# Row numbers and gates of an expert's slots: summed by TensorE, finished on ScalarE, with turns and sums at other places of the tile loop

## The chip, the cores and the metric

The kernel runs on one core of one Trainium2 chip. The metric is the device time of one execution in microseconds; three runs of the kernel before took 1885.34, 1885.52 and 1890.42 us (median 1885.52).

## The reference

One decoder layer over 512 tokens of width 1024, in float32: a mixing part (retention and dilated attention), then a mixture of experts, then a last RMSNorm. What matters here is the mixture. Each token goes to the top 4 of 32 experts by a softmax router; the gates are the softmax over the four values. An expert is a matrix of 1024x2048, a clamped SwiGLU, and a matrix of 1024x1024, and the results are summed into the tokens with the gates:

```
u   = xb @ w1[e] + b1[e]
glu = minimum(u[:, ::2], 7);  lin = clip(u[:, 1::2], -7, 7)
a   = glu * sigmoid(1.702 * glu) * (lin + 1)
y[row_tok] += (a @ w2[e] + b2[e]) * row_gate
```

## The kernel before, in words

The mixing part, the output projection and the router come first and fill the time up to about 720 us; the 32 experts follow, and after them a loop for overflowing experts (it runs zero times here) and the last norm.

**Slots.** An expert works on slots, each of which holds one token. The two first experts are fixed, the others are sorted by their number of tokens; after that order `KIND` (line 30) gives each place of the loop 96 slots ("L") or 64 ("S"): LLLL, then LS fourteen times. A matmul in float32r of two parts (hi and lo) stands for a float32 product: for L three products a tile (x hi by w hi, x hi by w lo, x lo by w hi), 12 matmuls; for S the hi and the lo part of x lie side by side in 128 columns, so that two products, 8 matmuls, do, and the lower half is added to the upper one by a `fold` (ScalarE copies the lower half, TensorE adds it).

**Tiles.** The loop at line 1318 runs over 384 tiles of 128x2048 float32, 1 MB each: eight of kind "A" (first matrix, k=0 to 7) and four of kind "B" (second matrix, k=0 to 3) an expert. The order is A(e), then B(e-1), then A(e+1), and so on. All engines follow an order written out by hand: each engine executes its instructions in the order of the source. In tile i TensorE multiplies with tile i; then ScalarE makes w_hi of tile i+4 (`prep_hi`, line 1043), VectorE makes w_lo of tile i+3 (`prep_lo`, line 1049) and SyncE issues the load that takes the buffer just freed. There are nine load buffers, five for w_hi and four for w_lo. The other operations of tile i stand behind these two on their engines.

**What else hangs on the tiles** (line numbers of the kernel before):

- `slot_hot` (line 1141, VectorE): a one-hot matrix oh, token by slot, from the rank of each token in the expert. At k=3 (for e=0 at k=0, 2 and 5).
- `slot_sum` (line 1147, TensorE): oh times `aux`, whose columns hold for each token p, 128*t, 1 and three bfloat16 parts of the gate. One matmul of 6 columns for each of the four token tiles, into `psl`. At A k=7 for the expert two ahead.
- `slot_rows` (line 1154): ScalarE copies the six sums to `sl`; POOL computes the row number (an empty slot is sent to a spare row), turns it into an int32 `idx`, issues the gather `xg` of the token rows, and sums the gate's three parts into `gate`.
- `turn` and `turn_copy` (lines 1173 and 1119): TensorE turns 512 columns of the gathered rows `xg` (or of the activations `av`) into a PSUM tile `pt`; ScalarE copies its hi part, VectorE subtracts to get the lo part. `av` of the expert before at k=3 and 4, `xg` of the next one at k=5 and 6. `pt` and `psl` share two buffers.
- `evacuate` (line 1305): for S first the fold; then the sigmoid on ScalarE (`open_gates`), `linear` and `times_glu` on VectorE, which read the one PSUM tile `u`. At B k=0. `times_gate` follows at B k=2.
- `close` (line 1313): ScalarE scales y by the gate into `ys`, POOL issues a DMA that adds the rows to `s_acc` in HBM. At A k=0 of the expert two later.

Of the kernel before, what the change touches and what calls it, by code (L numbers as in the profile page):

```python
# [17 lines left out]
OP = mybir.AluOpType  # L18
# [96 lines left out]
def body(tc, a, out):  # L115
# [679 lines left out]
    rg = rt.tile([P, NT, 2, E], F32, name="rg")  # L795
    rk1 = rg[:, :, 0]
    rkp = rt.tile([P, NT, E], F32, name="rkp")
    aux = rt.tile([P, NT, E, 6], BF, name="aux")
    selb = rt.tile([P, NT, 4, E], BF, name="selb")
    trib = rt.tile([P, 2, P], BF, name="trib")  # L800
    btile = rt.tile([P, TB], F32R, name="btile")
# [4 lines left out]
    V.memset(trib[:, 1], 1.0)  # L806
    V.tensor_copy(aux[:, :, :, 0], misc[:, 256:257].to_broadcast([P, NT * E]).rearrange("p (t e) -> p t e", t=NT))
    for t in range(NT):
        G.memset(aux[:, t, :, 1], float(P * t))
    G.memset(aux[:, :, :, 2], 1.0)  # L810
    s4 = ExitStack()
    psx = ExitStack()
    psB = psx.enter_context(tc.tile_pool(name="psB", bufs=2, space=PSUM, reuse_waits="tile"))
# [144 lines left out]
        A.activation(e4s[:, t0:t1], e4s[:, t0:t1], AF.Exp)  # L958

    def gate_parts(g, rest, s):  # L960
        V.tensor_copy(aux[:, :, s, 3], g)
        V.tensor_tensor(rest, g, aux[:, :, s, 3], op=OP.subtract)
        V.tensor_copy(aux[:, :, s, 4], rest)
        V.tensor_tensor(aux[:, :, s, 5], rest, aux[:, :, s, 4], op=OP.subtract)
# [138 lines left out]
    def slots_of(e):  # L1103
        return CAP if KIND[e] == "L" else SMALL
# [42 lines left out]
    def slot_sum(oh, aux_e):  # L1147
        n = oh.shape[2]
        ps = psC.tile([CAP, 8], F32, name="psl", tag="pt", bufs=2)
        for t in range(NT):  # L1150
            PE.matmul(ps[:n, :6], oh[:, t], aux_e[:, t], start=(t == 0), stop=(t == NT - 1))
        return ps[:n]

    def slot_rows(ps, fetch_rows=True):
        n = ps.shape[0]
        sl = m2.tile([CAP, 10], F32, name="sl")[:n]
        A.activation(sl[:, :6], ps[:, :6], AF.Copy)  # L1157
        G.tensor_scalar(sl[:, 6:7], sl[:, 2:3], misc[:n, 258:259], misc[:n, 257:258], op0=OP.mult, op1=OP.add)  # L1158
        G.tensor_add(sl[:, 7:8], sl[:, 0:1], sl[:, 1:2])
        idx = m2.tile([CAP, 1], I32, name="idx", bufs=4)[:n]  # L1160
        G.tensor_add(sl[:, 9:10], sl[:, 6:7], sl[:, 7:8])
        G.tensor_copy(idx, sl[:, 9:10])
        xg = None
        if fetch_rows:
            xg = m2.tile([CAP, D], F32, name="xg", bufs=1)[:n]
            G.indirect_dma_start(out=xg, out_offset=None, in_=xn2,
                                 in_offset=bass.IndirectOffsetOnAxis(ap=idx[:, :1], axis=0))
        G.tensor_add(sl[:, 8:9], sl[:, 3:4], sl[:, 4:5])
        gate = m2.tile([CAP, 1], F32, name="gate", bufs=4)[:n]
        G.tensor_add(gate, sl[:, 8:9], sl[:, 5:6])  # L1170
# [127 lines left out]
    U, Y, AVS, SG, AT, SL = {}, {}, {}, {}, {}, {}  # L1298
    now = {}
    hot_at = {(0, 0): 1, (0, 2): 0}  # L1300
    hot_at.update({(e, 3 if e else 5): e + 2 for e in range(E - 2)})
    sum_at = {(0, 1): 1, (0, 4): 0}
    sum_at.update({(e, 7): e + 2 for e in range(E - 2)})

    def evacuate(e):
        if KIND[e] == "S":
            fold(U[e], now["low"])
        u = U.pop(e)[:slots_of(e)]
        SG[e] = open_gates(u)
# [7 lines left out]

    for i, (kind, e, k) in enumerate(tiles):
        hi, lo = his.pop(i), los.pop(i)
        nx = sum_at.get((e, k)) if kind == "A" else None  # L1320
        if kind == "A":
            if nx is not None:
                now["ps"] = slot_sum(now["oh"], aux[:, :, nx])
            if e == 0 and k == 1:
                sort_rows()
                rgT = sort_turn()
            if e == 0 and k == 3:
                sort_tables(rgT)
            if e and k in (3, 4):
                now["at", k - 3] = turn(AVS[e - 1], k - 3)  # L1330
            if e + 1 < E and k in (5, 6):
                now["xt", k - 5] = turn(SL[e + 1][2], k - 5)
            if k == 0:
                U[e] = u_tile()
                if KIND[e] == "L":
                    for j in range(4):
                        bias_mm(U[e][:CAP, j], e, j)
            if KIND[e] == "L":
                xh, xl = X[e]
                for s_, m_ in ((xh, hi), (xh, lo), (xl, hi)):  # L1340
                    for j in range(4):
                        PE.matmul(U[e][:CAP, j], s_[:, k], m_[:, j * 512:(j + 1) * 512], start=False,  # L1342
                                  stop=(k == KC - 1 and s_ is xl))
            else:
                for m_ in (hi, lo):
                    for j in range(4):
                        PE.matmul(U[e][:, j], X[e][2][:, k], m_[:, j * 512:(j + 1) * 512], start=(k == 0 and m_ is hi),  # L1347
                                  stop=False, skip_group_check=True)
                    if k == 0 and m_ is hi:
                        for j in range(4):  # L1350
                            bias_mm(U[e][:SMALL, j], e, j, False)
        else:
            if k == 0:
                Y[e] = y_tile()
                if KIND[e] == "L":
                    for n in range(2):
                        bias_mm(Y[e][:CAP, n], e, 4 + n)
                if e == E - 1:
                    for q in range(2):
                        turn_copy(turn(AVS[e], q), slice(4 * q, 4 * q + 4), AT[e])  # L1360
            if KIND[e] == "L":
                ah, al = AT[e]
                for s_, m_ in ((ah, hi), (ah, lo), (al, hi)):
                    for c in range(2):
                        for n in range(2):
                            col = c * 1024 + n * 512
                            PE.matmul(Y[e][:CAP, n], s_[:, 2 * k + c], m_[:, col:col + 512], start=False,  # L1367
                                      stop=(k == 3 and s_ is al and c == 1))
            else:
                for m_ in (hi, lo):  # L1370
                    for c in range(2):
                        for n in range(2):
                            col = c * 1024 + n * 512
                            PE.matmul(Y[e][:, n], AT[e][2][:, 2 * k + c], m_[:, col:col + 512],  # L1374
                                      start=(k == 0 and c == 0 and m_ is hi), stop=False, skip_group_check=True)
                        if k == 0 and c == 0 and m_ is hi:
                            for n in range(2):
                                bias_mm(Y[e][:SMALL, n], e, 4 + n, False)
            if e == 0 and k == 0:
                ld = overflow_list()  # L1380
        prep_hi(i + AHEAD_HI)
        prep_lo(i + AHEAD)
        if kind == "A":
            if nx is not None:
                SL[nx] = slot_rows(now["ps"], nx > 0)
            if e == 0 and k == 0:
                sort_counts()
            if (e, k) in hot_at:
# [3 lines left out]
                AVS[0] = times_gate(SG.pop(0), AVS[0])  # L1392
            if e > 1 and k == 0:
                close(e - 2)
            if e and k in (3, 4):
                if k == 3:
                    AT[e - 1] = at_tiles(e - 1)
                turn_copy(now["at", k - 3], slice(4 * (k - 3), 4 * (k - 3) + 4), AT[e - 1])
            if e + 1 < E and k in (5, 6):
                if k == 5:  # L1400
                    X[e + 1] = x_tiles(e + 1)
                turn_copy(now["xt", k - 5], slice(4 * (k - 5), 4 * (k - 5) + 4), X[e + 1])
            if k == KC - 1:
                if KIND[e] == "S":
                    now["low"] = lower(U[e])
                if e == 0:
                    evacuate(0)
            if e == 3 and k == 2:
                G.dma_start(lb.rearrange("p a b -> p (a b)"), bcast(ld, 0, 4 * E))
            if e == 5 and k == 2:  # L1410
                V.tensor_copy(li, lb[0:1])
        else:
            if e + 1 < E:
                if k == 0:
                    evacuate(e + 1)
                if k == 2:
                    AVS[e + 1] = times_gate(SG.pop(e + 1), AVS[e + 1])
                    if e + 1 == E - 1:
                        AT[e + 1] = at_tiles(e + 1)
# [17 lines left out]
    with tc.For_i(0, extra) as it:  # L1437
# [94 lines left out]
```

## Time and profile before

| what | us |
|---|---|
| median of three runs | 1885.52 |
| the profiled execution | 1888.8 |
| its span, first to last instruction | 1887.0 |
| TensorE busy (matmul) | 1747.2 |
| VectorE busy | 1465.3 |
| ScalarE busy | 1084.0 |
| POOL busy | 651.0 |

The mean granted clock of TensorE is 0.966 of full speed. In the profile PE is TensorE's matmuls and PEld its weight loads (they overlap), DVE is VectorE, ACT is ScalarE, POOL is GpSimd and SP is SyncE, which only issues DMAs. L1178 is line 1178 of the kernel. `out<-in` names the tiles that an instruction writes and reads, `xN` counts the instructions put together in a row. Matmuls are pipelined, so that their durations overlap.

### The profile page before, as it was taken

How to read it: one execution, taken by the hardware profiler on the slowest of the kernel's cores; microseconds unless marked ns; L12 is line 12 of the kernel's file. 1: busy time of each engine (PE TensorE's matmuls, PEld its weight loads, DVE VectorE, ACT ScalarE, POOL GpSimd, SP SyncE). 2: the span in 40 equal slices, each digit the busy share in tenths (PEclk: the TensorE clock that was granted, in tenths of full speed). 3: DMA queues.
4: the chain of work that ended last, by engine and by line, in shares of the span. 5: the costliest groups of instructions: out<-in, count | busy, mean ns of one | idle time of the engine just before them, and what ended most of it. 6: DMA issues, size and time to landing. Idle time of an engine off the chain costs nothing.

```text
span 1887.0 us, 23253 instructions
## 1 busy us (share of the span) xinstructions
PE 1747.2 (93%) x8369; PEld 1327.1 (70%) x8369; DVE 1465.3 (78%) x1490; ACT 1084.0 (57%) x1000; POOL 651.0 (34%) x409
## 2 busy tenths in 40 slices
PE   5989999999999988999979999999999999999992
PEld 3878889888778875776656666666667667667661
DVE  7465535657663567998978998998999989999994
ACT  5232332222222334777867877877787787787781
POOL 2140001001110032022945256744746425844601
PEclk8999999999999998999989999999999999999996
DMA  9613424433573737899989999999999999999983
GB/s 313 165 52 90 112 74 139 149 114 105 150 199 119 243 155 276 313 391 361 391 310 389 370 371 396 377 381 378 386 381 383 384 389 369 399 380 373 383 315 116
DMA packets 207909, 525.47 MB, mean 278 GB/s; under 512 B 12102, under 2 KB 127222, under 8 KB 174896
## 3 DMA queue, kind: packets, MB, share of 16 engines
q1 hardware_dynamic: 197744, 494.99, 71.1%
q0 software_dynamic: 10048, 28.98, 6.3%
q8 instruction: 67, 1.10, 0.2%
q14 instruction: 50, 0.41, 0.1%
HBM read 503.67 MB, written 20.25 MB: 278 GB/s over the span
## 4 chain that ended last, share of the span: by engine, by line
PE 81%; DVE 9%; issue 5%; POOL 2%; DMA 2%; ACT 1%; SPq 0%; DVEq 0%; POOLq 0%; ACTq 0%
PE u L1342 21%; PE y L1367 10%; PE u L1347 8%; PE pp L213 6%; PE pp L215 6%; PE pp L214 6%; PE y L1374 5%; DVE w_lo L1049 3%; PE pp L247 2%; PE pp L245 2%; PE pp L246 2%; PE pt L1178 2%; PE u L1138 1%; POOL s_acc L1219 1%; PE y L740 1%
## 5 line engine op out<-in xcount | busy, mean ns | idle before, releaser
L1049 DVE TENSOR_TENSOR w_lo<-w_moe,w_hi 128x2048 fp32r<-128x2048 f32 x384 | 862.3, 2279 | 16.9 <-ACT sl L1157 10.7
L1043 ACT ACTIVATE w_hi<-w_moe 128x2048 fp32r<-128x2048 f32 x384 | 729.2, 1914 | 203.8 <-PE u L1342 116.2
L1219 POOL DMA_INDIRECT s_acc<-ys,idx x32 | 258.9, 8090 | 251.2 <-ACT ys L1218 235.6
L1342 PE MATMUL u<-w_hi,x 128*96 128x512 f32 x1152 | 317.5, 403 | 0.0
L1342 PEld LDWEIGHTS u<-w_hi,x 128*96 128x96 f32 x1152 | 181.5, 164 | 72.8 <-issue 0.6
L1158 POOL TENSOR_SCALAR sl<-sl,misc 96x1 f32<-96x1 f32 (+1 forms) x32 | 105.8, 3305 | 327.4 <-ACT sl L1157 327.4
L213 PE MATMUL pp<-hTh,w_hl 128*128 128x512 f32 x400 | 160.3, 401 | 0.0
L1342 PE MATMUL u<-w_lo,x 128*96 128x512 f32 x576 | 158.8, 398 | 0.0
L215 PE MATMUL pp<-hTh,w_hl 128*128 128x512 f32 x400 | 156.6, 391 | 0.0
L214 PE MATMUL pp<-hTl,w_hl 128*128 128x512 f32 x400 | 156.5, 391 | 0.0
L1367 PE MATMUL y<-w_hi,at 128*96 128x512 f32 x576 | 151.3, 396 | 0.0
L204 DVE TENSOR_TENSOR w_hl<-w_raw,w_hl 128x1024 fp32r<-128x1024 f32 (+1 forms) x66 | 91.3, 1397 | 72.3 <-ACT w_hl L203 72.3
L1347 PE MATMUL u<-w_hi,x 128*128 128x512 f32 x448 | 136.2, 427 | 0.0
L1347 PE MATMUL u<-w_lo,x 128*128 128x512 f32 x448 | 126.3, 405 | 0.6 <-DVE w_lo L1049 0.6
L1342 PEld LDWEIGHTS u<-w_lo,x 128*96 128x96 f32 x576 | 94.8, 165 | 41.2 <-issue 0.5
L1367 PEld LDWEIGHTS y<-w_hi,at 128*96 128x96 f32 x576 | 91.7, 161 | 44.4 <-issue 5.9
L203 ACT ACTIVATE w_hl<-w_raw 128x1024 fp32r<-128x1024 f32 (+1 forms) x66 | 65.2, 1002 | 70.7 <-PE pp L215 54.1
L278 POOL DMA_DIRECT2D s_mod<-brow x16 | 7.9, 492 | 281.1 <-DVE brow L275 228.4
L1347 PEld LDWEIGHTS u<-w_lo,x 128*128 128x128 f32 x448 | 88.1, 197 | 22.5 <-DVE w_lo L1049 1.2
L1347 PEld LDWEIGHTS u<-w_hi,x 128*128 128x128 f32 x448 | 82.9, 200 | 19.0 <-issue 5.4
L213 PEld LDWEIGHTS pp<-hTh,w_hl 128*128 128x128 f32 x400 | 75.5, 189 | 18.1 <-issue 2.6
L215 PEld LDWEIGHTS pp<-hTh,w_hl 128*128 128x128 f32 x400 | 75.4, 188 | 16.2
(345 smaller groups left out, 2901.9 us busy)
## 6 DMA issues: line engine op xcount, KB each, us to landing
w_moe<-in_w_mlp SPq DMA_DIRECT2D x384, 1024.0 KB, 7.6
w_raw<-in_w_in SPq DMA_DIRECT2D x76, 512.0 KB, 5.4
w_ada<-in_w_ada SPq DMA_DIRECT2D x24, 1024.0 KB, 6.2
w_raw<-in_w_ret_o SPq DMA_DIRECT2D x8, 512.0 KB, 4.4
w_o<-in_w_o SPq DMA_DIRECT2D x4, 1024.0 KB, 4.9
s_acc<-z POOLq DMA_DIRECT2D x5, 512.0 KB, 7.2
xin<-in_x SPq DMA_DIRECT2D x4, 512.0 KB, 6.6
w_raw<-in_w_att_o SPq DMA_DIRECT2D x8, 256.0 KB, 5.9
```

What stands on the lines that cost most here:

```text
L204: eng.tensor_tensor(lo[:, :kc], raw, hi[:, :kc].bitcast(F32), op=OP.subtract)
L213: PE.matmul(ps, hi[:, k], mh[:, k], start=(k == 0), stop=False)
L214: PE.matmul(ps, hi[:, k], ml[:, k], start=False, stop=False)
L215: PE.matmul(ps, lo[:, k], mh[:, k], start=False, stop=(k == kc - 1))
L1043: A.activation(his[i], loaded[i], AF.Copy)
L1049: V.tensor_tensor(los[i], loaded[i], his[i].bitcast(F32), op=OP.subtract)
L1158: G.tensor_scalar(sl[:, 6:7], sl[:, 2:3], misc[:n, 258:259], misc[:n, 257:258], op0=OP.mult, op1=OP.add)
L1219: G.indirect_dma_start(out=acc, out_offset=bass.IndirectOffsetOnAxis(ap=idx[:, :1], axis=0), in_=ys, in_offset=None, compute_op=OP.add)
L1342: PE.matmul(U[e][:CAP, j], s_[:, k], m_[:, j * 512:(j + 1) * 512], start=False, stop=(k == KC - 1 and s_ is xl))
L1347: PE.matmul(U[e][:, j], X[e][2][:, k], m_[:, j * 512:(j + 1) * 512], start=(k == 0 and m_ is hi), stop=False, skip_group_check=True)
L1367: PE.matmul(Y[e][:CAP, n], s_[:, 2 * k + c], m_[:, col:col + 512], start=False, stop=(k == 3 and s_ is al and c == 1))
L1374: PE.matmul(Y[e][:, n], AT[e][2][:, 2 * k + c], m_[:, col:col + 512], start=(k == 0 and c == 0 and m_ is hi), stop=False, skip_group_check ...
```

## The change

`aux` gets nine columns in three groups of three, so that a slot's row number parts, its flag and the gate's parts come to stand in the same three columns: (p, 1, gate part 1), (128*t, 0, gate part 2), (0, 0, gate part 3). TensorE adds the three groups into three sums: row, flag and gate. ScalarE computes the row number of the spare row from the flag, adds the row and writes int32, and copies the gate; POOL only issues the gather. The slot sum moves from A k=7 (expert two ahead) to B k=1 (expert three ahead), the one-hot from k=3 to k=5, the turns to k=2, 3 and k=6, 7. `evacuate` is split: the sigmoid of an L expert stands at the end of its A k=7, ahead of the second turn copy of the next expert's rows; the fold and the sigmoid of an S expert stay at B k=0, and its `linear` and `times_glu` move to B k=1.

```diff
-    aux = rt.tile([P, NT, E, 6], BF, name="aux")
+    aux = rt.tile([P, NT, E, 9], BF, name="aux")
...
-        G.memset(aux[:, t, :, 1], float(P * t))
-    G.memset(aux[:, :, :, 2], 1.0)
+        G.memset(aux[:, t, :, 3], float(P * t))
+    G.memset(aux[:, :, :, 1], 1.0)
+    for c in (4, 6, 7):
+        G.memset(aux[:, :, :, c], 0.0)
...
         for t in range(NT):
-            PE.matmul(ps[:n, :6], oh[:, t], aux_e[:, t], start=(t == 0), stop=(t == NT - 1))
+            for g in range(3):
+                PE.matmul(ps[:n, :3], oh[:, t], aux_e[:, t, 3 * g:3 * g + 3], start=(t == 0 and g == 0),
+                          stop=(t == NT - 1 and g == 2))
...
-        A.activation(sl[:, :6], ps[:, :6], AF.Copy)
-        G.tensor_scalar(sl[:, 6:7], sl[:, 2:3], misc[:n, 258:259], misc[:n, 257:258], op0=OP.mult, op1=OP.add)
-        G.tensor_add(sl[:, 7:8], sl[:, 0:1], sl[:, 1:2])
+        A.activation(sl, ps[:, 1:2], AF.Identity, scale=misc[:n, 258:259], bias=misc[:n, 257:258])
         idx = m2.tile([CAP, 1], I32, name="idx", bufs=4)[:n]
-        G.tensor_add(sl[:, 9:10], sl[:, 6:7], sl[:, 7:8])
-        G.tensor_copy(idx, sl[:, 9:10])
+        A.activation(idx, ps[:, 0:1], AF.Identity, bias=sl)
+        gate = m2.tile([CAP, 1], F32, name="gate", bufs=4)[:n]
+        A.activation(gate, ps[:, 2:3], AF.Copy)
...
-        G.tensor_add(sl[:, 8:9], sl[:, 3:4], sl[:, 4:5])
-        gate = m2.tile([CAP, 1], F32, name="gate", bufs=4)[:n]
-        G.tensor_add(gate, sl[:, 8:9], sl[:, 5:6])
...
-    hot_at.update({(e, 3 if e else 5): e + 2 for e in range(E - 2)})
-    sum_at = {(0, 1): 1, (0, 4): 0}
-    sum_at.update({(e, 7): e + 2 for e in range(E - 2)})
-
-    def evacuate(e):
+    hot_at.update({(e, 5): e + 2 for e in range(E - 2)})
+    sum_at = {("A", 0, 1): 1, ("A", 0, 4): 0, ("A", 0, 7): 2}
+    sum_at.update({("B", e, 1): e + 3 for e in range(E - 3)})
+
+    def open_u(e):
         if KIND[e] == "S":
             fold(U[e], now["low"])
+        SG[e] = open_gates(U[e][:slots_of(e)])
+
+    def close_u(e):
         u = U.pop(e)[:slots_of(e)]
-        SG[e] = open_gates(u)
         AVS[e] = linear(u)
         times_glu(u, AVS[e])
...
-            if e and k in (3, 4):
-                now["at", k - 3] = turn(AVS[e - 1], k - 3)
-            if e + 1 < E and k in (5, 6):
-                now["xt", k - 5] = turn(SL[e + 1][2], k - 5)
+            if e and k in (2, 3):
+                now["at", k - 2] = turn(AVS[e - 1], k - 2)
+            if e + 1 < E and k in (6, 7):
+                now["xt", k - 6] = turn(SL[e + 1][2], k - 6)
...
             if k == KC - 1:
                 if KIND[e] == "S":
                     now["low"] = lower(U[e])
+                else:
+                    open_u(e)
                 if e == 0:
-                    evacuate(0)
+                    close_u(0)
+            if e + 1 < E and k in (6, 7):
+                if k == 6:
+                    X[e + 1] = x_tiles(e + 1)
+                turn_copy(now["xt", k - 6], slice(4 * (k - 6), 4 * (k - 6) + 4), X[e + 1])
...
             if e + 1 < E:
-                if k == 0:
-                    evacuate(e + 1)
+                if k == 0 and KIND[e + 1] == "S":
+                    open_u(e + 1)
+                if k == (KIND[e + 1] == "S"):
+                    close_u(e + 1)
```

## Rows read from the trace of the kernel before

**Rows 1.** The page: busy time, share and instructions of each engine.
```profile
PE 1747.2 (93%) x8369; PEld 1327.1 (70%) x8369; DVE 1465.3 (78%) x1490; ACT 1084.0 (57%) x1000; POOL 651.0 (34%) x409
```

**Rows 2.** Stretches: us; PE, PEld, DVE, ACT, POOL busy; clock; DMA share; GB/s.
```profile
848.40:885.10 36.70, 36.70 (x172) 25.51 (x171) 32.72 (x21) 26.33 (x20) 10.60 (x8) 1.00 0.99 372
...
1391.84:1460.72 68.88, 65.07 (x300) 45.99 (x299) 64.45 (x41) 54.74 (x41) 44.99 (x16) 1.00 1.01 385
1460.72:1530.43 69.71, 66.37 (x300) 47.12 (x299) 64.45 (x41) 54.85 (x41) 26.03 (x16) 0.98 1.00 380
...
1388.30:1410.90 22.60, 18.79 (x91) 13.93 (x90) 22.60 (x15) 19.14 (x16) 12.57 (x2) 1.00 0.99 363
1410.90:1423.70 12.80, 12.80 (x55) 8.43 (x54) 12.09 (x9) 10.46 (x6) 12.08 (x6) 1.00 1.02 397
1423.70:1449.30 25.60, 25.60 (x122) 17.34 (x121) 23.41 (x16) 17.48 (x14) 16.70 (x4) 1.00 1.02 395
1449.30:1457.20 7.90, 7.90 (x36) 6.29 (x35) 6.37 (x5) 7.68 (x5) 3.64 (x7) 1.00 1.02 399
```

**Rows 3.** Waits of TensorE, 885 to 1810 us: total us, times, longest.
```profile
PE pt L1178 <- DVE at L1121: 41.5, 17, 3.3
PE pt L1178 <- DMA xg<-s_h,idx: 7.0, 1, 7.0
```

**Rows 4.** Timeline at A(S): start us, us, engine, instruction, [idle before, releaser].
```profile
1391.49 11.09 DVE L1049 TENSOR_TENSOR w_lo<-w_moe,w_hi 128x2048 fp32r<-128x2048 f32 x5
...
1402.84 0.55 DVE L1121 TENSOR_TENSOR at<-pt,at 128x384 fp32r<-128x384 f32 x1
...
1403.44 0.55 PE L1178 MATMUL pt<-misc,xg 96*128 96x96 f32 x4 [3.34 <-DVE at L1121]
```

**Rows 5.** Timeline at the end of A(L) and in B(S).
```profile
1444.97 0.36 ACT L1120 ACTIVATE x<-pt 128x256 fp32r<-128x256 f32 x1
...
1445.37 0.42 DVE L1121 TENSOR_TENSOR x<-pt,x 128x256 fp32r<-128x256 f32 x1 [0.73 <-ACT x L1120]
...
1446.27 0.31 PE L1151 MATMUL psl<-aux,oh 128*96 128x6 bf16 x4
...
1448.29 0.15 ACT L1157 ACTIVATE sl<-psl 96x6 f32<-96x6 f32 x1
...
1451.34 1.00 ACT L1200 ACTIVATE sg<-u 96x1024 f32<-96x1024 f32 x1
...
1452.24 5.51 ACT L1043 ACTIVATE w_hi<-w_moe 128x2048 fp32r<-128x2048 f32 x3
1452.25 1.00 POOL L1166 DMA_INDIRECT xg<-s_h,idx  x1 [0.56 <-POOL idx L1162]
1452.38 1.22 DVE L1205 TENSOR_SCALAR av<-u 96x1024 f32<-96x1024 f32 x1 [1.49 <-ACT sg L1200]
```

**Rows 6.** Timeline of POOL behind a gather in B(L).
```profile
1418.21 8.56 POOL L1168 TENSOR_TENSOR sl<-sl 64x1 f32<-64x1 f32 x1
```

**Rows 7.** Chain of waits: first matmuls of A(S), and one gather.
```profile
896.18 0.92 PE u L1347 x4
...
940.03 10.83 DMA xg<-s_h,idx
...
970.30 0.93 PE u L1347 x4
...
1804.65 0.93 PE u L1347 x4
```

**Rows 8.** DMA: packets 1391.84 to 1530.43 us; issues, size, median us to landing.
```profile
DMA packets 9721, 53.01 MB, mean 382 GB/s; under 512 B 896, under 2 KB 896, under 8 KB 5615
...
w_moe<-in_w_mlp SPq DMA_DIRECT2D x384, 1024.0 KB, 7.6
s_acc<-ys,idx POOLq DMA_INDIRECT x32, 18.0
xg<-s_h,idx POOLq DMA_INDIRECT x31, 7.4
```

More of the change, by code (lines that the diff above doesn't have):

```diff
@@ L960, in gate_parts @@
     def gate_parts(g, rest, s):
[L961 to L964, printed above, removed]
+        V.tensor_copy(aux[:, :, s, 2], g)
+        V.tensor_tensor(rest, g, aux[:, :, s, 2], op=OP.subtract)
+        V.tensor_copy(aux[:, :, s, 5], rest)
+        V.tensor_tensor(aux[:, :, s, 8], rest, aux[:, :, s, 5], op=OP.subtract)
     def gates(t0, t1):
@@ L1155, in slot_rows @@
         n = ps.shape[0]
-        sl = m2.tile([CAP, 10], F32, name="sl")[:n]
-        A.activation(sl[:, :6], ps[:, :6], AF.Copy)
-        G.tensor_scalar(sl[:, 6:7], sl[:, 2:3], misc[:n, 258:259], misc[:n, 257:258], op0=OP.mult, op1=OP.add)
-        G.tensor_add(sl[:, 7:8], sl[:, 0:1], sl[:, 1:2])
+        sl = m2.tile([CAP, 1], F32, name="sl")[:n]
+        A.activation(sl, ps[:, 1:2], AF.Identity, scale=misc[:n, 258:259], bias=misc[:n, 257:258])
         idx = m2.tile([CAP, 1], I32, name="idx", bufs=4)[:n]
-        G.tensor_add(sl[:, 9:10], sl[:, 6:7], sl[:, 7:8])
-        G.tensor_copy(idx, sl[:, 9:10])
+        A.activation(idx, ps[:, 0:1], AF.Identity, bias=sl)
+        gate = m2.tile([CAP, 1], F32, name="gate", bufs=4)[:n]
+        A.activation(gate, ps[:, 2:3], AF.Copy)
         xg = None
@@ L1319, in body @@
         hi, lo = his.pop(i), los.pop(i)
-        nx = sum_at.get((e, k)) if kind == "A" else None
+        nx = sum_at.get((kind, e, k))
+        if nx is not None:
+            now["ps"] = slot_sum(now["oh"], aux[:, :, nx])
         if kind == "A":
-            if nx is not None:
-                now["ps"] = slot_sum(now["oh"], aux[:, :, nx])
             if e == 0 and k == 1:
@@ L1382, in body @@
         prep_lo(i + AHEAD)
+        if nx is not None:
+            SL[nx] = slot_rows(now["ps"], nx > 0)
         if kind == "A":
-            if nx is not None:
-                SL[nx] = slot_rows(now["ps"], nx > 0)
             if e == 0 and k == 0:
@@ L1394, in body @@
                 close(e - 2)
-            if e and k in (3, 4):
-                if k == 3:
+            if e and k in (2, 3):
+                if k == 2:
                     AT[e - 1] = at_tiles(e - 1)
[L1398 to L1402, printed above, removed]
+                turn_copy(now["at", k - 2], slice(4 * (k - 2), 4 * (k - 2) + 4), AT[e - 1])
             if k == KC - 1:
@@ L1443, in body @@
         V.tensor_scalar(rke, rkp[:, :, ds(sv, 1)].rearrange("p t o -> p (t o)"), bo, None, op0=OP.subtract)
-        axe = m1.tile([P, NT, 6], BF, name="axe")
+        axe = m1.tile([P, NT, 9], BF, name="axe")
         V.tensor_copy(axe, aux[:, :, ds(sv, 1), :].rearrange("p t o c -> p t (o c)"))
```

## The prediction

> **What bounds the kernel now.** I read the busy line first, then busy time stage by stage, then what TensorE waited for, then the order of time around its longest wait, then the chain. The busy line [rows 1] gives TensorE 93% and VectorE 78% of the span, an average over unlike stages. The stages to look at are the experts. With a 96-slot expert after a 96-slot expert, TensorE is busy for 36.70 of 36.70 us and VectorE for 32.72: TensorE bounds. From the fifth expert on, 96-slot (L) and 64-slot (S) experts alternate, and a pair of them takes 68.88 or 69.71 us, of which TensorE works 65.07 or 66.37 and VectorE 64.45 [rows 2]. Neither is full; they take turns at waiting. I write A(L), B(L), A(S), B(S) for the eight tiles of the first and the four of the second projection of each kind; the order is A(L), B(S), A(S), B(L), in 25.60, 7.90, 22.60 and 12.80 us, and only A(S) has TensorE idle: 18.79 of 22.60 [rows 2].
>
> What it waits for is one thing: 41.5 us in 17 waits, turning rows (L1178) until VectorE has made the low part of an earlier turn (L1121) [rows 3]. In order of time [rows 4]: VectorE runs five w_lo back to back from 1391.49 for 11.09 us (2.2 each), then the subtraction for the first turn of the activations at 1402.84, and at 1403.44 TensorE, 3.34 us late, can turn the gathered rows, since the two psl/pt buffers are shared and that subtraction frees the first. VectorE's subtraction for tile k stands behind w_lo of tile k+3; TensorE asks for the buffer two tiles later, so it waits for a w_lo that it doesn't need yet. In every second pair the granted clock is 0.98 instead of 1.00, and those are the pairs of 69.71 us [rows 2].
>
> **The change part by part.** *Turns at k=2, 3 and 6, 7 (before 3, 4 and 5, 6).* A buffer is now asked for four tiles after its last use, when w_lo of the tile in hand must be there anyway. The 3.34 us wait and the two of about 0.24 behind it go. What is late next is VectorE, so I follow its chain. Take T=0 at the start of B(S).
>
> *Sigmoid of L at the end of A, before the second turn copy of the rows.* Before, VectorE waited 1.49 us for it in B(S) k=0 [rows 5]. Now ScalarE at A(L) k=7 runs w_hi, then waits for the end of the tile, then the sigmoid (1.00), and behind it stands the copy of the turned rows (0.36), for which VectorE's subtraction (0.42) waits [rows 5]. That is a new wait: queued behind the sigmoid are that copy and the next w_hi. With 0.2 us from TensorE to ScalarE the subtraction ends at T=1.9; VectorE has by then idled about 2.2 us. w_lo to 4.1, linear 1.22 [rows 5] and glu of the same size 1.22, so glu ends at T=6.5, where before it was 1452.38+2.44-1449.3=5.5.
>
> *From there VectorE has no wait until glu of S,* which now stands at B(L) k=1 (before k=0) and frees the single u tile for the next A(L). The work between: 14 w_lo (4 in B(S), 8 in A(S), 2 in B(L)) of 2.2 = 30.8; linear and glu twice, 4.8; one gate multiply of the size of linear, 1.2; four subtractions for 96 slots at 0.5 from [rows 4], 2.0; one one-hot compare, the 0.26 between the five w_lo and 1402.84, 0.3. Sum 39.1. Then TensorE must run A(L), 25.6 less the 0.2 of the slot sum that leaves it, 25.4 [rows 2, 5], with 0.1 to hand over; then the sigmoid, copy and subtraction close the ring, 0.2+1.00+0.36+0.42=2.0. The ring is 39.1+0.1+25.4+2.0=66.6 us a pair. The two other rings are shorter: VectorE's own work 64.45, TensorE's 65.07+0.7. In this walk TensorE waits some 0.4 us for w_lo in each of the last three tiles of A(S) and 0.9 for u in A(L) k=0, short waits in place of a long one.
>
> *Slot sum in three matmuls a tile, 12 instead of 4.* Four take 0.31 us with their drain [rows 5], at most 0.08 each; eight more are between 0 (if loads overlap) and 0.6. I take 0.04 each, half of it, as the last end is drain: 0.35 an expert. In pairs it lies beside the VectorE ring and costs nothing; its cover is the 0.8 us between TensorE's 65.8 and 66.6, gone if VectorE gets faster. In the L stage it is on the path: 7 sums, 2.4 us.
>
> *Row number and gate on ScalarE.* Six small POOL operations an expert go; one of 0.2 us took 8.56 beside w_lo [rows 6]. They are off the path (POOL 34% busy), except once: 7.0 us of waiting for gathered rows [rows 3], whose gather the chain shows landing late, 10.83 us from 940.03 [rows 7]. ScalarE gets two operations more, like the 0.15 us copy [rows 5]; form and int32 output are not in the trace, so 0.15 to 0.4 each. Hidden: ScalarE is busy 54.74 of 68.88 [rows 2]. They stand at B k=1 behind w_hi, and queued behind them are w_hi and the copies. ScalarE also takes over POOL's wait for the scatter-add of four experts before (idx has four buffers), 18.0 us from issue to landing [rows 8]; nine tiles lie between, 22 us in the walk, so 4 us are spare.
>
> *Three more memsets and a wider aux* run on POOL long before the experts, beside the output projection; 0, below 1 us if seen. One-hot at k=5 feeds a sum four tiles on, as before: 0. *Last experts:* VectorE enters A of the last expert up to 1.0 us later and TensorE waits there already: +1.0.
>
> **Sum.** From 970.30 to 1804.65 are 12 pairs, 69.53 each; the pair before took 74.12 from 896.18 [rows 7]. 12x(69.53-66.6)+(74.12-66.6)=35.2+7.5=42.7 gained, 2.4+1.0 lost: 39.3. The profiled execution took 1888.8 us (span 1887.0 and 1.8 around it), so 1849.5; the median of the runs is 1885.52, 3.3 lower, so 1846.
>
> **The rivals.** *(a) The transfers bound.* Over two pairs the DMA moved 53.01 MB at 382 GB/s [rows 8] and the engines' busy share is already 1.00 to 1.01 [rows 2]. 26.5 MB in 66.6 us asks for 398 GB/s. For it: the share. Against it: at the same share A(L), B(L) and B(S) run at 395 to 399 for 46 us [rows 2], a weight tile lands 7.6 us after issue [rows 8] with nine tiles in the ring, and no wait of ScalarE on a weight transfer shows. Held at 385 GB/s a pair would take 68.9: 12x0.6+5.2-3.4=9 us gained, 1876. The Trainium skill (SBUF — State Buffer, A bandwidth-pool intuition that's wrong) gives about 358 GB/s from HBM to a core; by that a pair would need 74 us, and nothing could be won. The trace does not agree: 382 GB/s are measured [rows 8].
>
> *(b) Slower: the gather for S's partner is shut out.* In B(S) ScalarE ends two w_hi (1.8 apart [rows 5]) and the small ones at T=5.4, and the gather starts 0.3 to 0.6 later, at 5.7 to 6.0. VectorE runs glu until 6.5, and then 6 w_lo and a gate multiply without a break to T=21. Beside linear a gather takes 1.00 us [rows 5], but the POOL operation that stood before a run of w_lo took 8.56 [rows 6]. If the index comes 0.5 us later than worked out, the gather goes out at 21, lands 7.4 later [rows 8] at 28.4, and A(S) k=6 wants it at 22.1: 6.3 us of waiting, less 1.3 of short waits that vanish, so 71.6 a pair: 13x71.6-908.5=+22, with +3.4 some 26 slower, 1911. Before, POOL's small operations waited themselves into the linear window; that shelter goes. The Trainium skill (SBUF — State Buffer, Who interferes with whom) says that a VectorE instruction with two SBUF inputs contends with a GpSimd instruction that reads SBUF, that one with a single SBUF input doesn't, and that the first to issue keeps the port to its end. By that rule a gather begun in glu is safe; the trace agrees as far as 1.00 beside linear and 8.56 beside w_lo go.
>
> *(c) The wait only moves:* VectorE is as late as before, pairs stay at 69.5, and only the 7 us gather wait goes: 1882 to 1885. For it: VectorE ends glu of L 1.0 us later. Against it: its idle time, 4.4 to 5.3 us a pair, has only the 2.2 us at A(L) k=7 left to sit in.
>
> **How the numbers follow.** The ring holds: 0.60, 1834 to 1860 (one us a pair either way is 13 us). (a), wholly or in part: 0.15, 1860 to 1878. (b): 0.16, 1892 to 1915. (c): 0.09, 1879 to 1886. What a measurement can tell from no change is 0.3%, 5.7 us. Faster: the ring and (a), 0.76; same: (c), 0.08; slower: (b) and what else stalls ScalarE, 0.16. The range 1833 to 1880 leaves out (b) and the slow end of (c).
>
> **What would show it.** Right: pairs of 66 to 67 us at clock 1.00; the wait of L1178 on L1121 down from 41.5 to under 10; VectorE waiting some 2 us for the copy at A(L) k=7 and TensorE about 1 us for u in A(L) k=0; L experts 0.3 longer; gathers of 1.0 us. Wrong: waits of TensorE on gathered rows, of ScalarE on weight tiles or on the scatter-add, or pairs of 69 and more.

## The result and the profile after

The changed kernel takes 1854.18 us (median of four runs, 1851.98 to 1856.01) against 1885.43 (1885.19 to 1890.42) for the kernel before on the same chip: a ratio of 0.982, 95% interval [0.981, 0.983]. The profiled execution took 1853.22 us with a span of 1851.4. Forecast were 1846, a range of 1833 to 1880, and 1834 to 1860 for the likeliest case.

The busy line of the page stands against [rows 1]:

```profile
PE 1750.5 (95%) x8625; PEld 1329.4 (72%) x8625; DVE 1457.3 (79%) x1490; ACT 1094.7 (59%) x1064; POOL 349.7 (19%) x220
```

POOL has half its work left; TensorE has 256 small matmuls more. The stretches of the kernel after stand against [rows 2]: one 96-slot expert after another, then pairs from the first matmul of A(S) to the next; the columns are those of [rows 2].

```profile
851.47:888.71 37.24, 37.24 (x180) 25.75 (x179) 32.69 (x20) 26.87 (x22) 13.97 (x2) 1.00 0.99 376
...
900.42:966.48 66.06, 64.79 (x313) 46.62 (x312) 60.53 (x39) 52.39 (x43) 31.85 (x5) 1.00 0.98 372
...
1365.45:1431.93 66.48, 66.05 (x315) 46.57 (x314) 63.99 (x41) 55.49 (x45) 13.23 (x5) 1.00 1.02 397
1431.93:1499.50 67.57, 65.85 (x315) 46.66 (x314) 64.09 (x41) 55.59 (x45) 12.57 (x5) 1.00 1.02 398
1499.50:1568.07 68.57, 67.45 (x315) 47.65 (x314) 64.27 (x41) 55.61 (x45) 14.43 (x5) 0.98 1.02 396
...
1701.02:1767.46 66.44, 65.31 (x303) 46.12 (x302) 63.02 (x40) 54.95 (x42) 11.03 (x4) 1.00 1.02 397
```

Most pairs that took 68.88 to 69.71 take 66.48, at a clock of 1.00. The 13 pairs from 900.42 to 1767.46 take 867.0 us; before they took 908.5 [rows 7]. That is 41.4 us gained. The way to the first pair is 4.4 us longer and the tail behind the last 1.4, which leaves the 35.6 us by which the spans differ.

What TensorE waits for, 885 to 1810 us (against [rows 3]), and under it the same of VectorE and ScalarE:

```profile
PE u L1195 <- ACT low L1190: 3.7, 4, 1.5
PE pt L1178 <- DVE av L1212: 2.9, 1, 2.9
PE u L1349 <- DVE w_lo L1051: 2.6, 11, 0.5
PE u L1140 <- DVE av L1209: 1.8, 7, 0.3
...
DVE x L1123 <- ACT x L1122: 35.7, 16, 3.2
...
ACT idx L1163 <- DMA s_acc<-ys,idx: 10.7, 1, 10.7
ACT w_hi L1045 <- DMA w_moe<-in_w_mlp: 8.9, 17, 1.7
```

The 41.5 us at L1178 are gone, and so is the 7.0 us wait for gathered rows. In their place VectorE waits 2.2 us a pair (35.7 in 16) for ScalarE's copy of the turned rows, and ScalarE waits for transfers, which it didn't before. The order of time at the end of A(L), in B(S) and in the A(S) behind it (against [rows 4, 5]):

```profile
1423.64 1.02 ACT L1200 ACTIVATE sg<-u 96x1024 f32<-96x1024 f32 x1 [1.38 <-PE u L1344]
1424.57 0.37 ACT L1122 ACTIVATE x<-pt 128x256 fp32r<-128x256 f32 x1
1424.97 0.43 DVE L1123 TENSOR_TENSOR x<-pt,x 128x256 fp32r<-128x256 f32 x1 [2.42 <-ACT x L1122]
1425.75 0.66 PE L1154 MATMUL psl<-aux,oh 128*96 128x3 bf16 x12
1428.44 0.34 ACT L1161 ACTIVATE sl<-psl,misc 96x1 f32<-96x1 f32 x1
1428.76 1.22 DVE L1209 SCALAR_TENSOR_TENSOR av<-u,av 96x1024 f32<-96x1024 f32 x1
1428.81 0.26 ACT L1163 ACTIVATE idx<-psl,sl 96x1 int32<-96x1 f32 x1
1429.33 7.05 POOL L1169 DMA_INDIRECT xg<-s_h,idx  x1 [26.74 <-PE y L1376]
1429.90 4.48 DVE L1051 TENSOR_TENSOR w_lo<-w_moe,w_hi 128x2048 fp32r<-128x2048 f32 x2
1434.30 1.27 DVE L1212 SCALAR_TENSOR_TENSOR av<-sg,top,av 96x1024 f32<-96x1024 f32 x1
1435.50 8.89 DVE L1051 TENSOR_TENSOR w_lo<-w_moe,w_hi 128x2048 fp32r<-128x2048 f32 x4
1445.58 0.49 PE L1178 MATMUL pt<-misc,xg 96*128 96x96 f32 x4
```

Sigmoid, copy, subtraction: VectorE's wait of 2.42 us is the wait that the walk foretold. The gather is the surprise: it starts while VectorE is still in glu, 0.57 us ahead of the next w_lo, and yet takes 7.05 us to issue instead of 1.00; it is through at 1436.38, 0.8 us behind the end of the gate multiply. TensorE turns the rows at 1445.58 without having waited. The DMA, 1365.45 to 1499.50 us, against [rows 8]:

```profile
DMA packets 9761, 53.29 MB, mean 398 GB/s; under 512 B 892, under 2 KB 892, under 8 KB 5628
...
w_moe<-in_w_mlp SPq DMA_DIRECT2D x48, 1024.0 KB, 15.8
xg<-s_h,idx POOLq DMA_INDIRECT x5, 13.7
```

The transfers do run at the 398 GB/s that the shorter pair asks for, but a weight tile now lands after 15.8 us instead of 7.6.

### The profile page after: what moved, and what is told of

The parts are those of the page before. It is cut to its first block, busy times and chain, and to the rows that moved or that the text cites. A ratio compares the mean times of both kernels' runs of the same rounds, so it can differ in the third digit from the quotient of the medians.

```text
span 1851.4 us, 23571 instructions
## 1 busy us (share of the span) xinstructions
PE 1750.5 (95%) x8625; PEld 1329.4 (72%) x8625; DVE 1457.3 (79%) x1490; ACT 1094.7 (59%) x1064; POOL 349.7 (19%) x220
## 4 chain that ended last, share of the span: by engine, by line
PE 74%; DVE 12%; DMA 7%; issue 4%; ACT 3%; SPq 0%; DVEq 0%; POOL 0%; ACTq 0%; POOLq 0%
PE u L1344 22%; DVE w_lo L1051 6%; PE pp L213 6%; PE pp L215 6%; PE pp L214 6%; PE y L1369 5%; PE u L1349 5%; PE y L1376 5%; DMA w_moe<-in_w_mlp 4%; DMA s_acc<-ys,idx 2%; PE pp L247 2%; PE pp L245 2%; PE pp L246 2%; PE pt L1178 2%; PE u L1140 2%
## 5 line engine op out<-in xcount | busy, mean ns | idle before, releaser
L1344 PE MATMUL u<-w_hi,x 128*96 128x512 f32 x1152 | 313.2, 402 | 0.1
L1169 POOL DMA_INDIRECT xg<-s_h,idx x31 | 145.9, 4705 | 669.7 <-ACT gate L1165 345.8
L204 DVE TENSOR_TENSOR w_hl<-w_raw,w_hl 128x1024 fp32r<-128x1024 f32 (+1 forms) x66 | 87.5, 1338 | 76.8 <-ACT w_hl L203 76.8
L1349 PE MATMUL u<-w_hi,x 128*128 128x512 f32 x448 | 128.9, 409 | 0.0
L1219 POOL DMA_INDIRECT s_acc<-ys,idx x32 | 97.3, 3040 | 164.7 <-ACT ys L1218 149.3
L1349 PEld LDWEIGHTS u<-w_lo,x 128*128 128x128 f32 x448 | 82.0, 188 | 34.3 <-DVE w_lo L1051 15.8
L1349 PEld LDWEIGHTS u<-w_hi,x 128*128 128x128 f32 x448 | 79.1, 188 | 19.9 <-issue 5.4
L214 PEld LDWEIGHTS pp<-hTl,w_hl 128*128 128x128 f32 x400 | 75.5, 189 | 14.6
```

Source lines behind the costliest of these rows:

```text
L204: eng.tensor_tensor(lo[:, :kc], raw, hi[:, :kc].bitcast(F32), op=OP.subtract)
L214: PE.matmul(ps, hi[:, k], ml[:, k], start=False, stop=False)
L1169: G.indirect_dma_start(out=xg, out_offset=None, in_=xn2, in_offset=bass.IndirectOffsetOnAxis(ap=idx[:, :1], axis=0))
L1219: G.indirect_dma_start(out=acc, out_offset=bass.IndirectOffsetOnAxis(ap=idx[:, :1], axis=0), in_=ys, in_offset=None, compute_op=OP.add)
```

## The experiments

The theory: the pair is now set by the ring through VectorE (its work, the sigmoid and the copy), and it needed both halves of the change, the placement for the gain and the arithmetic to keep POOL out of the way. The rivals: one half alone does it; or the transfers set the pair now.

**Placement alone, arithmetic left on POOL.** The kernel before, with the turns, sums, one-hots and sigmoid of the changed one:

```diff
-        A.activation(sl, ps[:, 1:2], AF.Identity, scale=misc[:n, 258:259], bias=misc[:n, 257:258])
-        A.activation(idx, ps[:, 0:1], AF.Identity, bias=sl)
+        A.activation(sl[:, :6], ps[:, :6], AF.Copy)
+        G.tensor_scalar(sl[:, 6:7], sl[:, 2:3], misc[:n, 258:259], misc[:n, 257:258], op0=OP.mult, op1=OP.add)
...
```

> Only the placement of the change (turns at k=2, 3, 6, 7, one-hot at 5, sum at B k=1, sigmoid and linear split); the slot sum is again four matmuls of six columns and POOL computes row number and gate as before. Theory (placement carries the gain, by freeing the turn buffer before TensorE asks): pairs of 66.5 us as with the whole change, the wait of L1178 on L1121 gone, and L experts 0.4 to 0.5 us shorter than with the whole change since eight matmuls an expert go; 1850 to 1856 us. Rival (the arithmetic had to leave POOL for the placement to work): behind the placement POOL's chain of four small operations starts at T=5.4, the last of them are shut out by the w_lo that starts at 6.5, the gather goes out after T=12 or after T=21, TensorE waits up to 6 us for gathered rows in A(S), pairs of 68 to 72 us, 1870 to 1910 us.

It takes 9.2% more than before, ratio [1.088, 1.097]; the profiled execution 2054.81 us. TensorE's waits, and one POOL operation between two rows of VectorE:

```profile
PE pt L1178 <- DMA xg<-s_h,idx: 188.9, 13, 18.6
```
```profile
1069.22 1.22 DVE L1209 SCALAR_TENSOR_TENSOR av<-u,av 96x1024 f32<-96x1024 f32 x1
...
1069.48 25.49 POOL L1159 TENSOR_TENSOR sl<-sl 96x1 f32<-96x1 f32 x1
...
1070.37 4.48 DVE L1049 TENSOR_TENSOR w_lo<-w_moe,w_hi 128x2048 fp32r<-128x2048 f32 x2
```

The wait for the turn buffer is gone here too, so the placement does take it away. But one addition of 96 numbers on POOL, which starts beside glu, now takes 25.49 us (0.18 before, when it fell into VectorE's idle time), the gather behind it goes out late, and TensorE waits 188.9 us for rows. That is the rival's mechanism at far more than its price of 1870 to 1910 us. At these places in the order the placement costs more than it gives unless the arithmetic leaves POOL.

**Arithmetic alone, everything at its old place.**

```diff
-    sum_at = {("A", 0, 1): 1, ("A", 0, 4): 0, ("A", 0, 7): 2}
-    sum_at.update({("B", e, 1): e + 3 for e in range(E - 3)})
+    sum_at = {(0, 1): 1, (0, 4): 0}
+    sum_at.update({(e, 7): e + 2 for e in range(E - 2)})
...
```

> Only the arithmetic of the change (nine columns, 12 matmuls, row number and gate on ScalarE); everything stands where it stood before. Theory: the turn wait of 3.3 us in A(S) stays, pairs of 68.9 to 69.7 us; the single wait of 7 us for gathered rows goes, L experts are 0.3 to 0.5 us longer; 1880 to 1888 us. Rival (POOL's shut-out operations were what cost): pairs fall to 67 us and below, 1855 us or less.

1912.4 us, ratio 1.013 [1.011, 1.015]: slower than before, which I hadn't expected. TensorE's waits:

```profile
PE pt L1178 <- DVE at L1123: 39.1, 17, 3.2
PE u L1195 <- ACT low L1190: 12.1, 1, 12.1
```

The turn-buffer wait stands, so the arithmetic alone gains nothing in the pairs. The 12.1 us are one wait at the first 64-slot expert, behind ScalarE's 14.6 us wait for the scatter-add whose row numbers it overwrites. An early pair (from 1112.03 us) takes 69.47 us, as before (69.58); two later ones take 71.35 and 71.54 at a clock of 0.95, and that is much of the rest of the loss. Why the clock fell there stays open.

**The sigmoid behind the copy (swap).** To take away VectorE's 2.2 us, the changed kernel with the second copy of the turned rows ahead of the sigmoid of L:

```diff
+            if e + 1 < E and k in (6, 7):
+                ...
+                turn_copy(now["xt", k - 6], slice(4 * (k - 6), 4 * (k - 6) + 4), X[e + 1])
             if k == KC - 1:
                 ...
                     open_u(e)
```

> The whole change, but at A(L) k=7 the sigmoid stands behind the second turn copy of the rows instead of ahead of it. Theory (the ring through the sigmoid sets 66.5 us; TensorE's own work of 66.0 is next): VectorE's wait of 2.4 us for the copy goes and glu of L ends 2 us earlier; pairs of 66.0 to 66.2 us, 4 to 6 us in all, 1847 to 1851 us. Rival (the weight transfers bind, 398 GB/s): pairs stay at 66.5 or more, ScalarE waits longer for weight tiles, landing stays at 15 us, 1852 to 1856 us. Second rival (only VectorE's order counts): pairs of 64.5 us, 1828 us.

2033.94 us, ratio 1.078 [1.076, 1.079], which lies in none of the expected ranges. TensorE's waits, and VectorE and POOL in order of time:

```profile
PE pt L1178 <- DMA xg<-s_h,idx: 181.2, 12, 15.7
```
```profile
1370.44 1.22 DVE L1209 SCALAR_TENSOR_TENSOR av<-u,av 96x1024 f32<-96x1024 f32 x1
1371.58 4.48 DVE L1051 TENSOR_TENSOR w_lo<-w_moe,w_hi 128x2048 fp32r<-128x2048 f32 x2
1373.16 23.79 POOL L1169 DMA_INDIRECT xg<-s_h,idx  x1 [21.57 <-ACT gate L1165]
1375.98 1.27 DVE L1212 SCALAR_TENSOR_TENSOR av<-sg,top,av 96x1024 f32<-96x1024 f32 x1
```

VectorE is through with glu 1.5 us before the gather starts instead of 0.6 after, and the gather is shut out for 23.79 us. This is the slower rival of the prediction, (b), above its price: up to 15.7 us of waiting a pair where 6.3 were put, and in all 147 us more than the kernel before where 26 were put (the mean granted clock, 0.933, is lower too). Between the two kernels lie 2 us in the order of gather and glu.

**Swap, with longer rows in the loads of the second matrix and six buffers for row numbers and gates.**

```diff
-                         w2[0, at].rearrange("o (k p) n -> p (o k) n", p=P)[:, 2 * k:2 * k + 2])
+                         w2[0, at].rearrange("o (k p c) n -> p (o k) c n", p=P, c=2)[:, k])
...
```

> The swap of e3_swap, and two things more: the second matrix is loaded in rows of 8 KB instead of 4 KB (a tile's two rows of a partition lie side by side, and the activations are turned in the matching order), and idx and gate have six buffers instead of four, so that ScalarE doesn't wait for the scatter-add of four experts before. Theory: the transfers take 0.7 us less of a pair (160 ns for 4 KB against 309 for 8 KB, eight tiles), landing falls below 15 us, the pairs that wait for weights (67.6 and 68.6 us) go, the 10.7 us wait of ScalarE in the first A(S) goes; 1845 to 1849 us, 2 to 5 us below e3_swap. Rival (TensorE binds anyway): the same time as e3_swap within 1 us.

2046.18 us, ratio 1.084 [1.082, 1.085]. The same shut-out (180.9 us of TensorE's waits on gathered rows in 12) drowns what the loads might do. The kernel is also 12 us slower than the swap alone, and no run here says why.

**Row numbers ahead of w_hi.** The three ScalarE operations go ahead of the tile's w_hi, so that the gather starts earlier:

```diff
+            SL[nx] = slot_rows(now["ps"], nx > 0)
...
         prep_hi(i + AHEAD_HI)
         prep_lo(i + AHEAD)
-        if nx is not None:
-            SL[nx] = slot_rows(now["ps"], nx > 0)
```

> The changed kernel with one move: the three ScalarE operations of the row number and gate (0.75 us) and the gather stand ahead of the tile's w_hi instead of behind it, about 1.8 us earlier. Theory A (a gather is shut out when it starts so late that VectorE has turned from linear and glu to w_lo): in B(S) it now starts inside linear, is issued in about 1.0 us instead of 7.05 and lands after about 7.5 us instead of 13.7. Since TensorE did not wait for it, the pairs stay at 66.5 us and the time at 1850 to 1856. Rival B (the place of the start decides nothing, any gather beside this stretch of VectorE waits for the gate multiply): issue stays at 7 us or more. Rival C (the 0.75 us ahead of w_hi cost): TensorE or VectorE waits for w_hi, pairs of 67 to 68, 1860 to 1875.

1861.16 us, ratio 0.986 [0.984, 0.988]. The gathers of 96-slot experts, 7.05 us in the changed kernel, go out in 0.93, so for them the start decides. Two timeline rows of this kernel show it from both sides; VectorE's linear ran from 1406.23 and from 1438.30:

```profile
1401.44 5.67 POOL L1169 DMA_INDIRECT xg<-s_h,idx  x1 [18.04 <-ACT gate L1165]
...
1438.33 0.93 POOL L1169 DMA_INDIRECT xg<-s_h,idx  x1 [24.93 <-PE y L1377]
```

The second starts beside linear; the first, of a 64-slot expert, starts 4.8 us ahead of it, beside a subtraction and 0.4 us before w_lo, and ends 0.9 us after linear has begun. The pairs are unchanged (66.47 us), as expected, but the kernel is slower than expected and than the changed one (the intervals of the two ratios don't overlap): ScalarE now waits 18.4 us in two waits for scatter-adds, and TensorE 8.9 in three around them.

**The same with 32 of the 384 loads left out** (every fourth tile of the second matrix multiplies with the tile before it; the output is not the layer's):

```diff
+    def again(i):
+        return i < len(tiles) and tiles[i][0] == "B" and tiles[i][2] == 3
...
+        if again(i):
+            loaded[i] = loaded[i - 1]
+            return
```

> As the first kernel of this set, but every fourth tile of the second projection multiplies with the tile before it again, so 32 of the 384 loads of 1 MB are left out (its output is not the layer's). All engines do the same work. Theory A (the ring through VectorE, the copy and the sigmoid sets the pair, the transfers only keep up): pairs stay at 66.5 us; the weights land in under 10 us instead of up to 15.8; the two long pairs of 67.6 and 68.6 us may go; at most 4 us less than the first kernel. Rival B (the transfers, 398 GB/s over a pair, set it): pairs of 65.5 to 66.1 us, 6 to 13 us less than the first kernel.

1858.97 us, ratio 0.985 [0.983, 0.986]: 2 us less than with all loads. Two pairs of this kernel:

```profile
1371.85:1438.33 66.48, 65.98 (x316) 46.50 (x315) 63.99 (x42) 55.38 (x45) 10.19 (x4) 1.00 0.98 363
1637.90:1704.37 66.47, 66.00 (x316) 46.53 (x315) 64.00 (x42) 55.40 (x45) 10.16 (x4) 1.00 0.98 369
```

At 363 to 369 GB/s, with weights landing after 7.3 us, the pair is 66.48 as before: the transfers don't set it. They made the few longer pairs, which are gone here.

**Swap, row numbers first, L's slot sum at k=0.** The swap again, with the gather early enough:

```diff
-    sum_at.update({("B", e, 1): e + 3 for e in range(E - 3)})
+    sum_at.update({("B", e, int(KIND[e + 3] == "S")): e + 3 for e in range(E - 3)})
```

> The swapped order (sigmoid of L behind the second copy of the turned rows), with the ScalarE operations ahead of w_hi and, for L experts, the slot sum at k=0 of the second projection instead of k=1: the gather starts some 6 us earlier than with the swap alone. Theory A (the swap alone cost 180 us only because the gather then began in a run of w_lo): gathers of S take about 1 us to issue, TensorE's wait for gathered rows is gone, and so is VectorE's 2.4 us wait for the copy; pairs of 66.0 to 66.5, 1847 to 1853. Rival B (the swap itself lengthens the pairs, by the later sigmoid): no wait for gathered rows, but pairs of 68 and more, 1875 or slower. Rival C (shut out at another place): TensorE waits for gathered rows again, over 1950.

1988.99 us, ratio 1.051 [1.048, 1.055]. No wait for gathered rows, as Theory A had it, and slow all the same, for a reason that no expectation named. ScalarE's waits, then POOL's groups (888 to 1800 us):

```profile
ACT idx L1163 <- issue: 211.9, 21, 11.8
```
```profile
L1219 POOL DMA_INDIRECT s_acc<-ys,idx x23 | 482.6, 20983 | 208.9 <-ACT ys L1218 115.0 <-PE pt L1178 52.4 <-PE u L1350 41.6
L1169 POOL DMA_INDIRECT xg<-s_h,idx x24 | 23.8, 993 | 209.5 <-ACT gate L1165 209.5
```

The shut-out has moved from the gather (0.99 us each) to the scatter-add (20.98). It reads its row numbers from one of four buffers, and ScalarE, which writes that buffer next, waits 10 us an expert with w_hi queued behind it. The same kernel with the 32 loads left out:

> As the second kernel of this set, with the same 32 loads of 1 MB left out (its output is not the layer's). Theory A (with the swap, VectorE's ring is shorter by its 2.4 us wait, so the transfers or TensorE set the pair): if the transfers do, pairs fall from about 66.4 to TensorE's 66.0, some 4 to 6 us less than the second kernel. Rival B (TensorE's 66.0 already sets it there): no difference above 3 us. Rival C (the ring of VectorE still sets it): both this and the second kernel at 66.5 or above.

1981.34 us, ratio 1.051 [1.047, 1.056]: no difference, ScalarE waiting as long. It couldn't tell anything of the transfers.

**Six buffers instead of four for row numbers and gates**, in three kernels on one chip: this one, the one with row numbers first, and the changed kernel.

```diff
-        idx = m2.tile([CAP, 1], I32, name="idx", bufs=4)[:n]
+        idx = m2.tile([CAP, 1], I32, name="idx", bufs=6)[:n]
...
-        gate = m2.tile([CAP, 1], F32, name="gate", bufs=4)[:n]
+        gate = m2.tile([CAP, 1], F32, name="gate", bufs=6)[:n]
```

> The swapped order with the row numbers first and L's slot sum at k=0, now with six buffers instead of four for the row numbers and gates. In the same kernel with four, ScalarE waited 212 us in 21 waits of about 11 before it wrote the row numbers, since the scatter-add that reads the buffer's old content was 20.8 us in issue. Theory A (that wait is all that made it slow): the wait goes, the scatter-adds may go on taking 20 us unseen, TensorE no longer waits for w_hi; pairs of 66.0 to 66.5 and 1846 to 1853. Rival B (POOL works in order, so that a scatter-add shut out for 20 us now holds the next gather): TensorE waits for gathered rows, over 1900. Rival C (the later sigmoid lengthens the ring): pairs of 68 to 70, 1875 to 1890.

> The changed kernel with the three ScalarE operations ahead of w_hi, now with six buffers for row numbers and gates. With four, that kernel took 1861 us, its pairs were those of the changed kernel (66.5), and ScalarE waited 18.4 us in two waits for scatter-adds at the start of the alternating experts, beside which TensorE waited 8.9. Theory A (those two waits are the whole difference): they go, 1850 to 1854. Rival B (the operations ahead of w_hi cost something in other places): 1858 or more.

> The changed kernel with six buffers instead of four for row numbers and gates, and nothing else. It shows one wait of ScalarE for a scatter-add, 10.7 us, behind which VectorE waited 5.4 and TensorE 1.2. Theory A (the cover of ScalarE ahead of TensorE swallows nearly all of it): 1 to 3 us less than the changed kernel's 1854, which is hardly to be told from no change. Rival B (the wait delays the first of the alternating pairs by more than TensorE's own waits show): 5 us less or more, below 1849.

The swap takes 1845.19 us (1844.17 to 1846.75), ratio 0.977 [0.976, 0.979]; row numbers first 1851.2, 0.981 [0.979, 0.983]; the changed kernel 1850.9 (1849.62 to 1852.75), 0.980 [0.979, 0.982]. So the scatter-add wait was what was wrong with the first two: the swap falls by 144 us and is now the fastest. On this chip all its runs lie below all those of the changed kernel; the intervals of the two ratios, which share the runs of the kernel before, touch at 0.979. For the changed kernel itself the wait was worth little: its interval overlaps with that of four buffers. Pairs of the swap, and then its chain of waits behind 1226 us:

```profile
986.00:1051.05 65.05, 65.05 (x316) 46.76 (x315) 64.10 (x41) 55.17 (x45) 32.66 (x5) 1.00 1.02 393
...
1247.98:1316.22 68.24, 66.66 (x315) 47.71 (x315) 64.56 (x41) 55.84 (x45) 33.52 (x5) 0.97 1.02 396
```
```profile
1226.99 15.02 DMA w_moe<-in_w_mlp
...
1242.12 1.92 ACT w_hi L1045
1244.04 0.37 ACT x L1122
...
1244.44 1.88 ACT low L1190
...
1246.36 1.14 PE u L1195 x4
```

With VectorE's wait for the copy down to 0.8 us (2.3 us in three waits up to 1181 us) TensorE has no gap: 65.05 of 65.05 us. A pair's 26.5 MB in 65.05 us would ask for 407 GB/s, and 396 are measured from 1181 us on; the landings grow to 16.7 us (median of 1181 to 1450 us), and from the third pair on the chain runs from a weight tile over w_hi and the fold's copy to TensorE. Rival (a) comes true one step later.

**The same with the 32 loads left out:**

> The swapped order with six buffers (1845 us), with every fourth tile of the second projection multiplied with the tile before it again, so that 32 of 384 loads of 1 MB are left out (its output is not the layer's). With all loads its first pairs took 65.03 to 65.05 us with TensorE without a gap; then the landing of a weight tile grew from 7 to 15 to 20 us and pairs came to 65.2 to 68.3, some with a granted clock of 0.97. Theory A (from there the transfers, 396 GB/s, set the pair, and the clock falls behind the gaps they make): all pairs at 65.05 and clock 1.00, weights landing in under 12 us, 1825 to 1830 us. Rival B (the long pairs come from elsewhere, from ScalarE or the clock by itself): long pairs stay, 1838 to 1845.

1827.6 us, ratio 0.968 [0.967, 0.969]: Theory A. The first and the last of its pairs:

```profile
988.09:1053.14 65.05, 65.05 (x316) 46.76 (x315) 64.10 (x41) 55.12 (x45) 31.68 (x5) 1.00 0.99 371
...
1638.53:1703.56 65.03, 65.03 (x315) 46.76 (x315) 64.10 (x41) 55.13 (x45) 32.06 (x5) 1.00 1.00 375
```

All eleven from 988.09 to 1703.56 are 65.04 on average, with no wait of TensorE on loads. So three rings lie close together: TensorE's 65.04, the transfers' 66 to 68, and in the changed kernel VectorE's 66.48.

## Why the prediction was right

**The turn-buffer wait goes.** It did, and it goes by the placement alone (the first experiment).

**The ring of 66.6 us a pair.** Measured 66.48, and it is VectorE's: with fewer loads it stays, with VectorE's wait for the copy cut to 0.8 it falls to 65.04. That wait was put at 2.2 us and is 2.2. TensorE's short waits were put at 2.1 a pair (three of 0.4 and one of 0.9); all that it loses is 1.4 (66.48 less the 65.04 of the last experiment), with the wait for u at 0.3. The forecast of these didn't fit itself: 65.8 of work and 2.1 of waits are 67.9, more than the ring. Nor does "every second pair" hold for the lower clock: between 1112 and 1739 us it is six pairs of nine. The sum used the mean of the pairs and doesn't hang on either.

**Slot sum.** Put at 0.35 us an expert; a 96-slot expert takes 37.24 instead of 36.70, so 0.54. The first experiment, which has four matmuls at the same place, separates it: from the third expert's first matmul to the fourth's it takes 36.23 us (787.69 to 823.92) where the changed kernel takes 36.68, so 0.45. Seven sums at 0.45 to 0.54 are 3.2 to 3.8 of the 4.4 us to the first pair (put at 2.4); what the remaining 0.6 to 1.2 are stays open.

**ScalarE's operations.** 0.34, 0.26 and 0.15 us, inside 0.15 to 0.4 each, and hidden.

**ScalarE's wait for the scatter-add, "4 us spare".** Not quite: one wait of 10.7 us at the first pair, because that scatter-add landed 32 us after its issue and not 18.0 [rows 8]. It delayed TensorE by 1.2. The delay came from POOL, where its issue took 24.41 us:

```profile
903.82 24.41 POOL L1219 DMA_INDIRECT s_acc<-ys,idx  x1 [2.63 <-ACT ys L1218]
```

The shut-out that the prediction weighs for the gather alone thus meets the scatter-add too, and the kernel before had shown it: its longest scatter-add issue took 21.88 us. The step was named and its price taken from a median; the experiments with four and six buffers show that it is the edge on which variants of this kernel fall.

**Tail.** 1.4 instead of 1.0.

**Rival (a), the transfers.** Partly true: the landings doubled, and the pairs above 66.48 cost 2.8 us (867.0 less 13 times 66.48). The Trainium skill (SBUF — State Buffer, A bandwidth-pool intuition that's wrong) gives about 358 GB/s; 398 are measured over 134 us, so this kernel, which runs on one core, doesn't bear the figure out as a ceiling.

**Rival (b), the gather shut out.** It came in part, without its condition. The index was not late: the gather started at T=5.9 (put at 5.7 to 6.0) and glu ended at 6.5, as worked out, but starting inside glu did not protect it. The Trainium skill (SBUF — State Buffer, Who interferes with whom) lets the first to issue keep the port; by that it should have gone out in 1 us, and the trace has 7.05. The kernel before could have told: the addition of 8.56 us [rows 6], which the prediction puts down to w_lo, had started inside glu as well, 0.64 us ahead of w_lo:

```profile
1417.71 1.22 DVE L1209 SCALAR_TENSOR_TENSOR av<-u,av 64x1024 f32<-64x1024 f32 x1
...
1418.85 4.47 DVE L1049 TENSOR_TENSOR w_lo<-w_moe,w_hi 128x2048 fp32r<-128x2048 f32 x2
```

What saved the forecast is that the gather got through at the gate multiply, at T=13, and not at 21: landed at 19.6, wanted at 22.1. With the swap it starts after glu, passes the gate multiply shut out, and (b) is there in full. The forecast was right by 2.5 us of slack that it hadn't counted on, and that part of it was luck.

**The signs.** The pairs, the clock of most of them, the vanished wait and VectorE's wait for the copy came as foretold. Gathers of 1.0 us, a sign of being right, did not, and the wait for u is 0.3 us rather than 1. Two signs of being wrong came, both small: ScalarE waited 10.7 us once for the scatter-add and 8.9 in 17 short waits for weight tiles.

**The 8 us between 1846 and 1854.** The pairs gave 1.3 us less than put (41.4 of 42.7), the first stage 2.0, the tail 0.4: 3.7 in the span. The other 4.3 are the step from the profiled execution to the median: the one before was 3.3 above its median, and the one after is 1.0 below its own.

## What to carry to other kernels

When a wait on a shared buffer goes, walk the rings that are left: here three lie within 3 us of each other, so the gain stops at the next one, and the one after that is the memory. An operation taken off a slow engine takes its waits along: ask how long the buffer that it overwrites is still being read, at the slowest reader and not at the median. And a small operation on POOL beside a busy VectorE has to start in a window; work out its start to half a microsecond, or move it so that it has more.

## What the runs showed of the hardware

A POOL operation that meets VectorE's instructions on two SBUF inputs can be held through many of them. Measured are an addition of 96 numbers at 25.49 us (0.18 in VectorE's idle time), an indirect gather at 23.79 (0.93 to 1.00 beside linear, which reads PSUM alone) and scatter-adds at 20.98 on average (1.42 for one at 1854.81 us of the kernel before, behind the experts).

Starting first doesn't protect it. Three operations that began beside glu, which reads PSUM and one SBUF tile, 0.6 to 0.9 us ahead of w_lo, were held all the same: the gather of the changed kernel 7.05 us, the addition of the kernel before 8.56, the addition of the first experiment 25.49.

It isn't as simple as that, though. In the changed kernel the gather got through at the gate multiply; with the swap the gather didn't, nor did the addition of the first experiment, and with the swap the short subtractions with a PSUM input, at 1386 and 1389 us, didn't let it through either. Nor is every start inside a run of w_lo held: the scatter-add at 1437.13 us of the changed kernel, in a run of four, took 1.94. Which boundary lets POOL in stays open; no run here tells it apart.

Twelve matmuls of 3 columns took 0.66 us together for 96 slots and 0.54 for 64, in place of 0.31 and 0.28 for four of 6 columns.
